# Hybrid decoder step on one core: the cache attention's value products moved into the next prompt block

## The chip, the core and the metric

The kernel runs on one core of one Trainium2 chip. TensorE (PE) multiplies matrices, VectorE (DVE), ScalarE (ACT) and GpSimd (POOL) do the element work, SyncE (SP), ACT and POOL issue transfers. The metric is the time of one execution in device microseconds (us); lower is better.

## The reference

One step of a two-layer decoder for a prompt of 1024 tokens and eight sample requests of one token each. Layer 0 is an mLSTM, layer 1 is multi-head latent attention over 8 heads, each followed by a dense feed-forward network. The change touches layer 1 alone, and there two things: the attention of the prompt over itself, and the attention of each sample over its cache of 8192 rows, which lie in pages at random places:

```python
def one_seq(args):
    ql, qr, cn, krn, pages = args
    c_all = jnp.concatenate([cache_latent[layer_idx, pages].reshape(past, KV_LORA), cn], axis=0)
    kr_all = jnp.concatenate([cache_k_rope[layer_idx, pages].reshape(past, QK_ROPE), krn], axis=0)
    s = jnp.einsum('qhc,kc->hqk', ql, c_all) + jnp.einsum('qhr,kr->hqk', qr, kr_all)
    s = jnp.where(mask, s.astype(jnp.float32) * MLA_SCALE, -jnp.inf)
    p = jax.nn.softmax(s, axis=-1)
    return jnp.einsum('hqk,kc->qhc', p.astype(c_all.dtype), c_all)
```

The cached latent rows (256 wide) serve as keys and, after the softmax, as values.

## The kernel before

**Prompt attention.** `attention` walks over 8 heads and, in each, over 4 blocks of 256 queries: 32 blocks, called slots (`slot = h * 4 + i`). `prompt(h, G, ...)` traces one block: the score matmuls (L1693 to L1700, into PSUM tiles `sc`), the softmax on DVE and ACT (L1701 to L1718), the transposes of the probabilities (L1731), their split into two float32r halves (`wh`, `wl`, L117, L118, and L128 to L130 where POOL helps) and the products with the values (L1751). Between blocks stand pieces of `head_ops(h + 1)`, which makes the next head's keys `kt` (matmuls of 512 columns, L134 to L136) and, for every second head, the values `vt` of two heads. Its weights come by SP into `swh` and `swl`, which have one buffer each: the load for the keys of an odd head can start when the last product with the value weights before it is done. The keys of the next head are made behind the first block of the current head.

**Cache attention.** `sample_units(b, first)` is a generator: each of the 8 samples is done in two units, 16 in all (numbered 0 to 15 below), and each unit in two halves (`u`), one half per slot, with no half in slots 0, 30 and 31 and two in 3, 11 and 27. A half gathers 2048 cache rows: POOL issues two indirect transfers of 1 MB into `nat` (L1840) and two small ones into `nrp` (L1841). DVE transposes them in 32 x 32 squares (L1848, five instructions of 1024 elements a partition), and PE multiplies them by the queries (L1855) into the left half of a PSUM tile `ss`. After the second half comes the unit's softmax on DVE and ACT (L1860 to L1871), 16 small copies that spread the probabilities over `pz` (L1876, half on DVE, half on ACT), and the value products (L1880, 32 matmuls, each of them two passes in the trace) into the right half of `ss`; DVE adds them to `acc` (L1881). After the second unit of a sample follows the merge: a chain of four small PE steps (L1887, L1892, L1897, L1904) with DVE and ACT steps in between.

**What sets the order.** A scheduler lays the traced instructions out, engine by engine, by its own model of when each is ready; each engine then works through its list in order and waits where an operand is late. Two handles steer it here. `high_priority(offset=SOON)` raises instructions, so that they are taken as soon as the model has them ready (the cache's scores and values). `issue_after(ins)` puts what a block traces behind `ins` on the same engine, with no wait for its end.

**Buffers that tie the units together.** `nat` has four buffers, so the gathers of unit n+2 wait for the value products of unit n. `ss` has two buffers. `pz`, `sS` and `acc` have one.

Of the kernel before, what the change touches and what calls it, by code (L numbers as in the profile page):

```python
# [12 lines left out]
AF = mybir.ActivationFunctionType  # L13
ALU = mybir.AluOpType
# [4 lines left out]
P = 128  # L19
# [72 lines left out]
class Kern:  # L92
# [15 lines left out]
    def t(self, pool, shape, tag, dt=F32, bufs=None):  # L108
        self.n += 1
        return pool.tile(shape, dt, tag=tag, name=f"{tag}{self.n}", **({"bufs": bufs} if bufs else {}))  # L110
# [1483 lines left out]
    def attention(self, ckh, ckl, kk, kl, cqp, cq):  # L1594
# [16 lines left out]
        ahead = {}  # L1611

# [10 lines left out]
        def head_ops(h):  # L1623
# [8 lines left out]
            yield r  # L1632
            for c in range(2):
                cs = slice(c * cw, (c + 1) * cw)
                ps = ps1()
                for j in range(2):
                    self.mm3(ps, wh[:, j], wl[:, j], ckh[:, j, cs], ckl[:, j, cs], j == 0, j == 1)
                split(kt[:, 0, cs], kt[:, 1, cs], ps, [P, cw])
# [29 lines left out]
        def prompt(h, G, kt, vt):  # L1668
# [10 lines left out]
            for i in (2 * G, 2 * G + 1):  # L1679
# [8 lines left out]
                for c in range(nb):  # L1688
# [10 lines left out]
                    if last:  # L1699
                        mm(o[:, w - P:], mk[:, 0], mk[:, 1], start=False, stop=True)  # L1700
# [17 lines left out]
                pn.append(px)  # L1718
            for j0 in range(0, nk, 4):
# [52 lines left out]
        for h in range(8):  # L1772
# [11 lines left out]
            for i, G in enumerate(range(4) if h % 2 == 0 or h == 7 else range(3, -1, -1)):  # L1784
# [8 lines left out]
                if slot == 30:  # L1793
                    next(units, None)
                    pr.release()
                    self.pc.release()
                    out = self.mla_out()
                    next(out)
# [15 lines left out]
    def sample_units(self, b, first):  # L1814
# [6 lines left out]
        psb = lambda: self.mmt("ss")  # L1821
# [7 lines left out]
        ss = psb()  # L1829
# [47 lines left out]
        with self.tc.high_priority(offset=SOON):  # L1877
            for i in range(8):
                for j in range(4):
                    nc.tensor.matmul(psV[32 * j:32 * j + 32], pz[:, j, i], keys[i // 4][:, j * 4 + i % 4], start=i == 0, stop=i == 7)  # L1880
        V.scalar_tensor_tensor(self.acc, self.acc, al, psV, op0=ALU.mult, op1=ALU.add)  # L1881
        if not first:

            ps = psb()
            m = t([P, 1], "m", 1)
            V.tensor_scalar(m, nb, -1.0, None, op0=ALU.mult)
            nc.tensor.transpose(ps[0:1, 0:P], m, self.ident)  # L1887
            mn = t([1, 8], "mn", 1)
            V.reduce_max(mn, ps[0:1, 0:P].rearrange("o (x h) -> o h x", h=8), axis=AX.X)
            mc = t([P, 256], "sS", 1)[0:1, :P].rearrange("o (x h) -> o x h", h=8)  # L1890
            V.tensor_copy(mc, mn.unsqueeze(1).to_broadcast([1, 16, 8]))
            nc.tensor.matmul(ps[:, P:P + 1], mc.rearrange("o x h -> o (x h)"), self.ones[0:1, 0:1], start=True, stop=True)  # L1892
            fac = t([P, 1], "fac", 2)
            V.tensor_tensor(fac, m, ps[:, P:P + 1], op=ALU.subtract)
            nc.scalar.activation(fac, fac, AF.Exp)
            V.tensor_scalar(self.lrow, self.lrow, fac, None, op0=ALU.mult)
            nc.tensor.matmul(ps[:, 256:257], self.ct[:, C_SL:C_SL + P], self.lrow, start=True, stop=True)  # L1897
            rl = t([P, 1], "rl", 2)
            V.reciprocal(rl, ps[:, 256:257])
            w = t([P, 8], "w0", 2)  # L1900
            V.tensor_scalar(w, self.ct[:, C_SL:C_SL + 8], rl, fac, op0=ALU.mult, op1=ALU.mult)
            ps = psb()
            for f in range(2):
                nc.tensor.matmul(ps[:, f * 8:f * 8 + 8], self.acc[:, f * P:(f + 1) * P], w, start=True, stop=True)  # L1904
            V.tensor_copy(self.olat[:, :, :, b], ps[:, 0:16].rearrange("p (f h) -> p f h", f=2))
# [164 lines left out]
```

## Time and profile before

| | |
|---|---|
| three timed runs | 2610.46, 2617.35, 2619.27 us (median 2617.35) |
| the profiled execution | 2606.56 us, span of its instructions 2604.6 us |
| PE busy | 2496.4 us, 96% of the span |
| DVE, ACT, POOL busy | 1858.4, 1327.5, 573.7 us |
| HBM traffic | 146 GB/s over the span |

The profiled execution is 0.4% under the median of the timed runs, so numbers of its trace are set against its own time. The stage that the change touches is the attention of layer 1, from about 1331 to 1810 us of the span. In rows of groups and of the timeline, "out<-in" names tiles, the number in brackets or behind the second bar is the time for which the engine sat idle just before, with what ended it.

### The profile page before, as it was taken

What the parts mean: (1) busy time and instruction counts of PE and PEld (TensorE: products, weight loads), DVE (VectorE), ACT (ScalarE), POOL (GpSimd) and SP (SyncE); (2) the same over time, 40 slices, a digit from 0 to 9 for tenths busy, and PEclk for the clock granted to TensorE, in tenths of its full rate; (3) what the DMA queues carried; (4) which work ended last, traced back from release to release, by engine and by line L of the source; (5) the groups of instructions that cost most, each with busy time, mean ns of one, the idle gap of its engine ahead of it and who ended that gap; (6) DMA issues with size and microseconds to landing.
All of it is one profiled execution on the core that took longest, in us unless ns stands there. A gap on an engine that the chain in (4) does not pass through costs nothing. (4 is left out here: it accounts for less than half of the span.)

```text
span 2604.6 us, 54290 instructions
## 1 busy us (share of the span) xinstructions
PE 2496.4 (96%) x21151; PEld 2361.3 (91%) x21151; DVE 1858.4 (71%) x4491; ACT 1327.5 (51%) x3281; POOL 573.7 (22%) x588
## 2 busy tenths in 40 slices
PE   8998988999999999999988888998999999999998
PEld 8998987999999999999977676777899999999998
DVE  4345669898777777666658776777498877777765
ACT  4122334456655656554445454656356656556543
POOL 1000102301111111112435445451211111111102
PEclk9999999999999999999999999999999999999999
DMA  6133555526666665555568667674635666665663
GB/s 195 41 64 82 150 140 126 162 74 135 119 129 124 129 129 115 113 154 165 177 230 290 219 222 249 223 254 127 206 106 111 119 129 129 129 128 115 121 139 112
DMA packets 343127, 382.87 MB, mean 147 GB/s; under 512 B 23465, under 2 KB 275502, under 8 KB 334550
## 3 DMA queue, kind: packets, MB, share of 16 engines
q0 software_dynamic: 58688, 180.35, 29.7%
q1 hardware_dynamic: 258982, 182.30, 23.5%
q10 hardware_dynamic: 25200, 16.75, 2.6%
q8 instruction: 166, 2.72, 0.4%
q14 instruction: 91, 0.75, 0.1%
HBM read 253.63 MB, written 125.70 MB: 146 GB/s over the span
## 5 line engine op out<-in xcount | busy, mean ns | idle before, releaser
L1187 POOL DMA_DIRECT2D x_d<-wl x72 | 86.8, 1205 | 996.1 <-DVE wl L1186 359.7
L117 ACT ACTIVATE wh<-wr 128x512 fp32r<-128x512 f32 (+2 forms) x167 | 133.3, 800 | 192.9 <-PE mm L135 111.4
L1848 DVE STREAM_TRANSPOSE tt<-nat 128x1024 f32<-128x1024 f32 x128 | 153.6, 1222 | 23.4 <-DMA nat<-in_cache_latent_dram,idx 13.8
L118 DVE TENSOR_TENSOR wl<-wr,wh 128x1024 fp32r<-128x1024 f32 (+2 forms) x80 | 92.9, 1162 | 37.3 <-ACT wh L117 36.3
L134 PE MATMUL mm<-zh,wh 128*128 128x344 f32 x320 | 104.2, 326 | 6.0 <-DVE ot L467 6.0
L117 ACT ACTIVATE b<-u 128x256 fp32r<-128x256 f32 (+1 forms) x252 | 98.5, 415 | 20.5 <-PE ss L136 6.3
L118 DVE TENSOR_TENSOR b<-u,b 128x256 fp32r<-128x256 f32 (+1 forms) x252 | 103.5, 424 | 6.8 <-ACT b L117 5.4
L1187 POOL DMA_DIRECT2D x_d<-st x72 | 104.4, 1450 | 4.8 <-DVE dC L118 3.8
L135 PE MATMUL mm<-zl,wh 128*128 128x344 f32 x320 | 103.8, 324 | 0.0
L136 PE MATMUL mm<-zh,wl 128*128 128x344 f32 x320 | 103.7, 324 | 0.0
L118 DVE TENSOR_TENSOR wh<-S,wh 128x512 fp32r<-128x512 f32 x108 | 74.6, 691 | 34.6 <-ACT wh L117 34.3
L1855 PE MATMUL ss<-tt,qbd 128*32 128x128 f32 x2560 | 86.6, 276 | 4.2 <-DVE tt L1848 2.3
L117 ACT ACTIVATE wh<-S 128x512 fp32r<-128x512 f32 x108 | 67.9, 629 | 44.4 <-PE sc L136 32.1
L1855 PEld LDWEIGHTS ss<-tt,qbd 128*32 128x32 f32 x2560 | 69.7, 110 | 16.8 <-DVE tt L1848 10.8
L1751 PE MATMUL mm<-wh,vt 128*128 128x256 f32 (+1 forms) x320 | 76.5, 301 | 7.5 <-ACT wh L117 5.5
L134 PE MATMUL sc<-zh,wh 128*128 128x344 f32 x256 | 82.6, 323 | 0.9 <-ACT wh L117 0.8
L136 PE MATMUL sc<-zh,wl 128*128 128x344 f32 x256 | 82.0, 320 | 0.7 <-DVE wl L118 0.7
L135 PE MATMUL sc<-zl,wh 128*128 128x344 f32 x256 | 81.9, 320 | 0.0
L1880 PE MATMUL ss<-nat,pz 128*32 128x256 f32 x1024 | 67.3, 393 | 12.3 <-ACT pz L1876 11.7
L1710 ACT ACTIVATE wr<-sc,mx,rqt 128x512 f32<-128x512 f32 (+2 forms) x96 | 64.3, 674 | 20.4 <-DVE mx L1705 10.0
L1840 POOL DMA_INDIRECT nat<-in_cache_latent_dram,idx x64 | 60.6, 947 | 62.6 <-PE ss L1880 49.0
L1751 PEld LDWEIGHTS mm<-wh,vt 128*128 128x128 f32 x320 | 56.6, 199 | 19.4 <-ACT wh L117 9.9
(1078 smaller groups left out, 10650.7 us busy)
## 6 DMA issues: line engine op xcount, KB each, us to landing
wr<-in_ffn_w_gate_up_dram SPq DMA_DIRECT2D x96, 512.0 KB
x_d<-st POOLq DMA_DIRECT2D x72, 520.0 KB, 8.0
x_d<-wl POOLq DMA_DIRECT2D x72, 512.0 KB, 6.0
dr<-in_ffn_w_down_dram SPq DMA_DIRECT2D x72, 256.0 KB
wr<-in_mlstm_w_in_dram SPq DMA_DIRECT2D x24, 512.0 KB
wr<-in_mlstm_w_out_dram SPq DMA_DIRECT2D x16, 512.0 KB
q<-qn_d SPq DMA_DIRECT2D x28, 256.0 KB
wr<-in_mla_w_o_dram SPq DMA_DIRECT2D x14, 512.0 KB
```

The lines of the kernel that those rows point to most:

```text
L117: ins = nc.scalar.activation(hi, src, AF.Copy)
L118: self.low = e.tensor_tensor(lo, src, hi.bitcast(F32), op=ALU.subtract)
L134: mm(ps, wh, xh, start=start, stop=False, **kw)
L135: mm(ps, wh, xl, start=False, stop=False, **kw)
L136: self.last = mm(ps, wl, xh, start=False, stop=stop, **kw)
L1187: nc.gpsimd.dma_start(self.x_d[:, 2 * dp:2 * dp + 2, 512 * i:512 * i + 2 * PW[i]], st[i], accum_op=ALU.add)
L1710: nc.scalar.activation(px[:, ks], o, AF.Exp, bias=mx[:, 0:1], scale=f, accum_out=sm[:, c:c + 1])
L1751: nc.tensor.matmul(o, x, y, start=i == 0, stop=i == len(ops) - 1)
L1840: nc.gpsimd.indirect_dma_start(out=nat[:, s].rearrange("p s c -> p (s c)"), out_offset=None, in_=lat, in_offset=ix)
L1848: V.transpose(out=tt, in_=src.rearrange("p s (c i) -> p c s i", i=32))
L1855: nc.tensor.matmul(psS[32 * j:32 * j + 32, u * P:u * P + P], self.qbd[:, b, cb], tt[:, c, 4 * j:4 * j + 4].rearrange("p s k -> p (s k)"), ...
L1880: nc.tensor.matmul(psV[32 * j:32 * j + 32], pz[:, j, i], keys[i // 4][:, j * 4 + i % 4], start=i == 0, stop=i == 7)
```

## The change

1. The value products and all that follows them in a unit (`acc`, the merge) become a function `values`, kept in `self.due`. It is called when the next prompt block has traced its scores and its softmax, just ahead of its transposes; if no block comes in between (the slots with two halves, slot 30), it is called at the start of the next half. 
2. The value matmuls stay raised and are also queued behind `self.qk`, the last score matmul of the newest block.
3. The merge no longer takes two PSUM tiles of its own; it uses parts of the unit's `ss`.
4. The keys of odd heads are made behind the second block of the head before, not behind the first (`if h % 2: yield`), and the key matmuls of all heads but the first are queued behind `self.qk`.

No matmul, copy or transfer is added or left out.

```diff
         late = []
         ahead = {}
+        self.due = None
...
             yield r
+            if h % 2:
+                yield
             for c in range(2):
                 cs = slice(c * cw, (c + 1) * cw)
                 ps = ps1()
                 for j in range(2):
-                    self.mm3(ps, wh[:, j], wl[:, j], ckh[:, j, cs], ckl[:, j, cs], j == 0, j == 1)
+                    with self.tc.issue_after(self.qk) if h else nullcontext():
+                        self.mm3(ps, wh[:, j], wl[:, j], ckh[:, j, cs], ckl[:, j, cs], j == 0, j == 1)
...
                     if last:
-                        mm(o[:, w - P:], mk[:, 0], mk[:, 1], start=False, stop=True)
+                        self.qk = mm(o[:, w - P:], mk[:, 0], mk[:, 1], start=False, stop=True).ins
...
                 pn.append(px)
+            if self.due:
+                self.due()
             for j0 in range(0, nk, 4):
...
                 if slot == 30:
                     next(units, None)
+                    if self.due:
+                        self.due()
                     pr.release()
...
-        psb = lambda: self.mmt("ss")
+        if self.due:
+            self.due()
         if first:
...
-        ss = psb()
+        ss = self.mmt("ss")
...
-        with self.tc.high_priority(offset=SOON):
-            for i in range(8):
-                for j in range(4):
-                    nc.tensor.matmul(psV[32 * j:32 * j + 32], pz[:, j, i], keys[i // 4][:, j * 4 + i % 4], start=i == 0, stop=i == 7)
-        V.scalar_tensor_tensor(self.acc, self.acc, al, psV, op0=ALU.mult, op1=ALU.add)
-        if not first:
-
-            ps = psb()
...
+        acc, lrow = self.acc, self.lrow
+
+        def values():
+            self.due = None
+            with self.tc.high_priority(offset=SOON), self.tc.issue_after(self.qk):
+                for i in range(8):
+                    for j in range(4):
+                        nc.tensor.matmul(psV[32 * j:32 * j + 32], pz[:, j, i], keys[i // 4][:, j * 4 + i % 4], start=i == 0, stop=i == 7)
+            V.scalar_tensor_tensor(acc, acc, al, psV, op0=ALU.mult, op1=ALU.add)
+            if not first:
...
+        self.due = values
         yield
```

The order that the scheduler makes of it shows at three places. In the rows, `ss` with a number is one unit's PSUM tile, `sc` the scores of a prompt block, `mm` a PSUM tile of transposes, products or keys. The new lines are 4 to 13 higher: L1697 to L1704 are scores, L1737 transposes, L1757 products of a prompt block, L1864 the cache's scores, L1893 its values.

PE at the value products of unit 4 (`ss_17795` before, `ss_17769` after). Before, they stand in the middle of the scores of unit 5 and of a prompt block's transposes and products:

```order
L1731 MATMUL mm_17900<-ct_66,wr_17870 128x128
L1731 MATMUL mm_17900<-ct_66,wr_17885 128x128 x2
L1698 MATMUL sc_18050<-kl_14540,qrr_17853 128x512
L1855 MATMUL ss_18148<-tt_18337,qbd_16086 32x128 x8
L1855 MATMUL ss_18148<-tt_18333,qbd_16086 32x128 x8
L1855 MATMUL ss_18148<-tt_18335,qbd_16086 32x128 x5
L1880 MATMUL ss_17795<-nat_17796,pz_15354 32x256 x16
L1880 MATMUL ss_17795<-nat_17924,pz_15354 32x256 x16
L1855 MATMUL ss_18148<-tt_18335,qbd_16086 32x128 x3
```

After, on the same engine, they follow the last score of a block (`sc_18044`) and precede its transposes:

```order
L1700 MATMUL sc_18037<-kk_14539,qrr_17827 128x512
L1702 MATMUL sc_18037<-kl_14540,qrr_17827 128x512
L1697 MATMUL sc_18044<-kt_16819,q_17826 128x256
L1698 MATMUL sc_18044<-kt_16819,q_17826 128x256
L1699 MATMUL sc_18044<-kt_16819,q_17826 128x256
L1700 MATMUL sc_18044<-kk_14539,qrr_17827 128x256
L1702 MATMUL sc_18044<-kl_14540,qrr_17827 128x256
L1704 MATMUL sc_18044<-mk_15350 128x128
L1893 MATMUL ss_17769<-nat_17770,pz_15354 32x256 x16
L1893 MATMUL ss_17769<-nat_17920,pz_15354 32x256 x16
L1737 MATMUL mm_18094<-ct_66,wr_18029 128x128
```

What moved: the values went behind more of the queue, from the middle of one group of small work to the gap between a block's scores and its transposes.

PE at the first scores of unit 8 (`ss_19289` before, `ss_19281` after), whose gathers wait for the values of unit 6. Before, they come behind the last step of the merge of unit 7 (L1897, L1904):

```order
L1897 MATMUL ss_19187<-lrow_18469,ct_66 128x1
L1694 MATMUL sc_19393<-kt_18532,q_19209 128x256
L1695 MATMUL sc_19393<-kt_18532,q_19209 128x256
L1696 MATMUL sc_19393<-kk_14539,qrr_19210 128x256
L1698 MATMUL sc_19393<-kl_14540,qrr_19210 128x256
L1700 MATMUL sc_19393<-mk_15350 128x128
L1751 MATMUL mm_19036<-wh_19017,vt_17399 128x128
L1904 MATMUL ss_19205<-w_19203,acc_18466 128x8
L1855 MATMUL ss_19289<-tt_19300,qbd_16086 32x128 x8
L1855 MATMUL ss_19289<-tt_19296,qbd_16086 32x128 x8
```

After, they come two dozen matmuls of a prompt block and the second-half scores of unit 7 behind the values of unit 6, inside the products of that block (`mm_18621`):

```order
L1704 MATMUL sc_18983<-mk_15350 128x128
L1697 MATMUL sc_18998<-kt_17653,q_18759 128x512
L1698 MATMUL sc_18998<-kt_17653,q_18759 128x512
L1757 MATMUL mm_18621<-wh_18602,vt_17631 128x128
L1699 MATMUL sc_18998<-kt_17653,q_18759 128x512
L1864 MATMUL ss_19281<-tt_19292,qbd_16086 32x128 x8
L1864 MATMUL ss_19281<-tt_19288,qbd_16086 32x128 x8
L1864 MATMUL ss_19281<-tt_19290,qbd_16086 32x128 x8
L1757 MATMUL mm_18621<-wl_18603,vt_17631 128x128
```

What moved: the first scores of a unit stand earlier, and nearer to the values of the unit two before it.

PE at the keys of head 5 (`mm_19426` before, `mm_19607` after). Before, they stand in the products of the first block of head 4, which use `vt_18905`:

```order
L1751 MATMUL mm_19416<-wl_19407,vt_18905 128x128
L1751 MATMUL mm_19416<-wh_19406,vt_18905 128x128
L1751 MATMUL mm_19416<-wl_19407,vt_18905 128x256
L1751 MATMUL mm_19416<-wh_19406,vt_18905 128x256
L134 MATMUL mm_19426<-ckh_14547,swh_19364 128x512
L135 MATMUL mm_19426<-ckl_14548,swh_19364 128x512
```

After, they stand behind the products of the second block (`mm_19591`):

```order
L1757 MATMUL mm_19591<-wh_19572,vt_18899 128x256
L1757 MATMUL mm_19591<-wh_19572,vt_19046 128x256
L1757 MATMUL mm_19591<-wl_19573,vt_19046 128x256
L1757 MATMUL mm_19591<-wh_19572,vt_19046 128x256
L134 MATMUL mm_19607<-ckh_14547,swh_19356 128x512
L135 MATMUL mm_19607<-ckl_14548,swh_19356 128x512
```

What moved: one block of a prompt lies between the last product with `vt` weights and the keys.

More of the change, by code (lines that the diff above doesn't have):

```diff
@@ L1876, in sample_units @@
                 e(pz[32 * kb:32 * kb + 32, j, :, 8 * kb:8 * kb + 8], pT[32 * j:32 * j + 32, kb])
-        with self.tc.high_priority(offset=SOON):
-            for i in range(8):
-                for j in range(4):
-                    nc.tensor.matmul(psV[32 * j:32 * j + 32], pz[:, j, i], keys[i // 4][:, j * 4 + i % 4], start=i == 0, stop=i == 7)
-        V.scalar_tensor_tensor(self.acc, self.acc, al, psV, op0=ALU.mult, op1=ALU.add)
-        if not first:
-            ps = psb()
[L1885 to L1905, printed above, removed]
@@ new lines, in sample_units @@
+        acc, lrow = self.acc, self.lrow
[7 more added lines that the diff above has]
+            if not first:
+                m = t([P, 1], "m", 1)
+                V.tensor_scalar(m, nb, -1.0, None, op0=ALU.mult)
+                nc.tensor.transpose(ss[0:1, 0:P], m, self.ident)
+                mn = t([1, 8], "mn", 1)
+                V.reduce_max(mn, ss[0:1, 0:P].rearrange("o (x h) -> o h x", h=8), axis=AX.X)
+                mc = t([P, 256], "sS", 1)[0:1, :P].rearrange("o (x h) -> o x h", h=8)
+                V.tensor_copy(mc, mn.unsqueeze(1).to_broadcast([1, 16, 8]))
+                nc.tensor.matmul(ss[:, P:P + 1], mc.rearrange("o x h -> o (x h)"), self.ones[0:1, 0:1], start=True, stop=True)
+                fac = t([P, 1], "fac", 2)
+                V.tensor_tensor(fac, m, ss[:, P:P + 1], op=ALU.subtract)
+                nc.scalar.activation(fac, fac, AF.Exp)
+                V.tensor_scalar(lrow, lrow, fac, None, op0=ALU.mult)
+                nc.tensor.matmul(ss[:, 256:257], self.ct[:, C_SL:C_SL + P], lrow, start=True, stop=True)
+                rl = t([P, 1], "rl", 2)
+                V.reciprocal(rl, ss[:, 256:257])
+                w = t([P, 8], "w0", 2)
+                V.tensor_scalar(w, self.ct[:, C_SL:C_SL + 8], rl, fac, op0=ALU.mult, op1=ALU.mult)
+                for f in range(2):
+                    nc.tensor.matmul(ss[:, 384 + f * 8:392 + f * 8], acc[:, f * P:(f + 1) * P], w, start=True, stop=True)
+                V.tensor_copy(self.olat[:, :, :, b], ss[:, 384:400].rearrange("p (f h) -> p f h", f=2))
```

## The prediction

> **What bounds the kernel now.** The page first, then the stage that the change touches, as one window (its ends and length, the busy time of PE, its weight loads, DVE, ACT and POOL, the granted clock, the DMA share and GB/s).
>
> ```profile
> span 2604.6 us, 54290 instructions
> ...
> PE 2496.4 (96%) x21151; PEld 2361.3 (91%) x21151; DVE 1858.4 (71%) x4491; ACT 1327.5 (51%) x3281; POOL 573.7 (22%) x588
> ```
> ```profile
> 1331.00:1810.00 479.00, 421.23 (x5230) 334.50 (x5228) 346.29 (x774) 265.43 (x700) 221.00 (x219) 0.96 0.66 229
> ```
>
> TensorE bounds the program. In the stage it is busy for 421.2 of 479.0 us, so it idles 57.8 us there, and its granted clock averages 0.96. The change adds and removes no work, so it can only move these idle times and the clock. What PE waits for, by groups of its instructions in the stage (idle before them behind the second bar), and four rows of who waited for whom (us, times, longest):
>
> ```profile
> L1855 PE MATMUL ss<-tt,qbd 128*32 128x128 f32 x2560 | 86.6, 276 | 4.2 <-DVE tt L1848 2.3 <-DVE sm L1713 0.5
> ...
> L1880 PE MATMUL ss<-nat,pz 128*32 128x256 f32 x1024 | 67.3, 393 | 12.3 <-ACT pz L1876 11.7 <-issue 0.4
> ...
> L1731 PE MATMUL mm<-ct,wr 128*128 128x128 f32 x273 | 49.2, 289 | 12.1 <-ACT spl L129 5.0 <-ACT wr L1715 4.0 <-ACT ot L1754 2.3
> ...
> L134 PE MATMUL mm<-ckh,swh 128*128 128x512 f32 x28 | 12.5, 447 | 5.6 <-DMA swh<-uw_d 4.6 <-ACT ot L1754 1.0
> ...
> L1904 PE MATMUL ss<-w,acc 128*128 128x8 f32 x32 | 5.2, 240 | 1.4 <-DVE w L1901 1.4
> ...
> L1892 PE MATMUL ss<-ones,sS 1*128 1x1 f32 x16 | 3.0, 256 | 1.0 <-DVE sS L1891 0.9
> ```
> ```profile
> POOL nat L1840 <- PE ss L1880: 49.0, 12, 6.5
> ...
> DVE tt L1848 <- DMA nat<-in_cache_latent_dram,idx: 13.8, 5, 4.1
> ...
> PE ss L1904 <- DVE w L1901: 1.4, 2, 0.7
> ...
> PE ss L1892 <- DVE sS L1891: 0.9, 1, 0.9
> ```
>
> The values (L1880) wait 11.7 us for `pz`, the keys 4.6 us for their weights. The first two rows of the waits show the return path: POOL's gathers wait for the values, DVE's transposes for the gathers. PE itself hardly waits for transposes (2.3 us).
>
> **Values later: the gain.** How much PE work covers a unit's softmax, I count in the two orders (instructions between its last score and its first value product) and price at the spacing of starts in a stretch at full clock; small matmuls by busy time over count, 86.6/2560 and 67.3/1024 us a pass.
>
> ```profile
> 1649.97 0.87 PE L1731 MATMUL mm<-ct,wr 128*128 128x128 f32 x6
> 1650.60 0.48 PE L1693 MATMUL sc<-kt,q 128*128 128x512 f32 x1
> 1650.92 0.40 PE L1694 MATMUL sc<-kt,q 128*128 128x512 f32 x1
> 1651.15 0.40 PE L1695 MATMUL sc<-kt,q 128*128 128x512 f32 x1
> ...
> 1658.49 0.28 PE L1751 MATMUL mm<-wl,vt 128*128 128x256 f32 x1
> 1658.61 0.40 PE L1751 MATMUL mm<-wh,vt 128*128 128x256 f32 x2
> ```
>
> That is 0.11 us a transpose, 0.23 for 512 columns, 0.12 for 256. Units 2 to 14 have 2.6 to 14.6 us of cover before and 9.5 to 28.2 after; I cost their waits at nothing then. Units 0, 1 and 15 gain none: 5.1 becomes 4.6, 4.6 becomes 4.5, 5.6 becomes 3.3.
>
> ```profile
> 1388.06 3.70 PE L1880 MATMUL ss<-nat,pz 128*32 128x256 f32 x62 [1.54 <-ACT pz L1876]
> ```
> ```profile
> 1494.73 5.36 PE L1880 MATMUL ss<-nat,pz 128*32 128x256 f32 x64 [3.78 <-ACT pz L1876]
> ```
> ```profile
> 1789.03 0.63 PE L1880 MATMUL ss<-nat,pz 128*32 128x256 f32 x4 [0.91 <-ACT pz L1876]
> ```
>
> Unit 0 keeps 1.5 + 0.5, unit 15 keeps 0.9 + 2.3, unit 1 gets 0.1: 5.3 us together. So 11.7 - 5.3 = **6.4 us saved**; at best 11.7, at worst nothing, if DVE and ACT are later with `pz` by as much.
>
> **Keys one block later: the gain.** The longest wait is that of head 5's keys:
>
> ```profile
> 1616.16 0.77 PE L134 MATMUL mm<-ckh,swh 128*128 128x512 f32 x1 [3.83 <-DMA swh<-uw_d]
> ```
>
> Their load starts when the last `vt` product ends and needs about that long. A whole block now lies between (two dozen matmuls or more, over 4 us), so **4.6 us** go. The splits of odd keys on POOL move with them and are needed two blocks later only. SP's loads keep their place, so no `q` load is queued behind a longer wait.
>
> **The clock.** The two longest waits, 3.78 and 3.83 us, are followed by slow stretches (granted clock third from the end of a row):
>
> ```profile
> 1616.10:1620.00 3.90, 3.84 (x9) 3.10 (x10) 0.00 (x0) 0.91 (x2) 0.00 (x0) 0.50 0.63 246
> ...
> 1494.70:1500.10 5.40, 5.37 (x74) 4.55 (x78) 3.79 (x5) 0.24 (x1) 1.15 (x2) 0.70 0.01 3
> ```
>
> 0.50 x 3.9 + 0.30 x 5.4 = **3.6 us** go with them. After the 1.54 us wait the 62 passes took 3.70 us, the usual 0.06 each, so short waits cost nothing more. I charge 1.8 us for each new wait of 3.8 us or longer. (The Trainium skill, "TensorE: Matmul & The Clock Gate", Part 1, puts the limit at an idle window of about 3.4 us, after which the clock is halved; that speaks against the change, since it would make some of the new waits below dearer. No wait here lies between 1.54 and 3.78 next to a measured clock to say where the limit is; by the page's figure the forecast is unchanged, since its only long wait is over both.)
>
> **Gathers later: the cost.** POOL issues the gathers of unit n+2 when the values of unit n have read the first `nat`, and the first scores of n+2 need both transfers and three transposes. Two such cases, each engine's timeline:
>
> ```profile
> 1498.65 0.96 POOL L1840 DMA_INDIRECT nat<-in_cache_latent_dram,idx  x1 [6.33 <-PE ss L1880]
> 1499.91 0.94 POOL L1840 DMA_INDIRECT nat<-in_cache_latent_dram,idx  x1 [0.30 <-issue]
> ```
> ```profile
> 1507.93 1.25 DVE L1848 STREAM_TRANSPOSE tt<-nat 128x1024 f32<-128x1024 f32 x1 [2.30 <-DMA nat<-in_cache_latent_dram,idx]
> ...
> 1509.19 1.24 DVE L1848 STREAM_TRANSPOSE tt<-nat 128x1024 f32<-128x1024 f32 x1
> ```
> ```profile
> 1555.94 0.48 DVE L1881 SCALAR_TENSOR_TENSOR acc<-acc,al,ss 128x256 f32<-128x256 f32 x1 [0.41 <-PE ss L1880]
> ...
> 1564.60 3.50 DVE L1848 STREAM_TRANSPOSE tt<-nat 128x1024 f32<-128x1024 f32 x3 [1.74 <-DMA nat<-in_cache_latent_dram,idx]
> ```
> ```profile
> DMA to landing us min/median/max: 5.6/7.4/9.9
> ```
>
> From the values' end (1494.73 + 5.36 = 1500.09) to the first transpose 7.8 us; in the second case (1555.9 to 1564.6) 8.7. With the middle, 8.3, two transposes of 1.24 and 0.4 for a small operation between, PE can start the scores **11.2 us** after the values' end. The work in between, by the orders, for n = 0 to 13: before 17.9, 15.0, 19.8, 16.7, 18.8, 23.3, 22.2, 23.2, 23.4, 15.7, 24.7, 15.5, 22.5, 17.1 us; after 11.5, 12.1, 8.4, 12.8, 10.8, 14.0, 5.9, 8.2, 9.6, 10.9, 8.2, 8.2, 9.6, 10.6. So the slack that hides the gathers today is gone. Real time runs longer than this count:
>
> ```profile
> L1855 PE MATMUL ss<-tt,qbd x2560: 270/273/423, 1367.0 to 1779.7; 128*32 128x128 f32 x197
> ```
> ```profile
> L1880 PE MATMUL ss<-nat,pz x1024: 376/379/636, 1388.1 to 1793.7; 128*32 128x256 f32 x171
> ```
>
> From 1367.0 to 1793.7 are 427 us, against 334 by the count: a factor 1.28, of which I keep 1.2, since some waits go. Times 1.2, only n = 2, 6, 7, 10 and 11 fall short of 11.2, by 1.1, 4.1, 1.4, 1.4 and 1.4: **9.4 us of new waits**, and **1.8** for the long one. With the factor 1 it is 21.6; with all transfers at the fastest landing 1.3. DVE stands in the same wait, and a block's reductions and splits behind it, but PE has stopped at the scores by then, so I count it once.
>
> **Merges.** In units 9, 13 and 15 two of the four joints now have only some six transposes or four scores of cover (0.6 to 1.1 us). The waits seen at such joints are 1.4 in two and 0.9 in one, 0.8 each: six of them, less the 2.4 seen today, **+2.4 us**; between -2.4 and +5. POOL's clearing of `acc` waits for the merge as before. The two PSUM tiles fewer cost nothing: the first scores of n+2 now wait only for unit n's own tile, whose merge is over by then.
>
> **Sum**: -6.4 - 4.6 - 3.6 + 9.4 + 1.8 + 2.4 = -1.0 us against the profiled 2606.6. The median of the runs is 10.8 above that; on its scale 2616.4, in round terms **2616 us**.
>
> **Rivals.** *Gathers in time (faster).* If both transfers land like the fastest (5.6 us after issue), the need is 1.25 + 5.6 - 1.4 + 2.9 = 8.4 us after the values' end, and only n = 6 waits, 1.3. Then -14.6 + 1.3 + 2.4 = -10.9, and if the values also fill three of the 4.0 us for which transposes wait for the softmax (L1731, `wr`), -14: **2603 us**. For it: fewer transfers may share the time; against it: the median landing. (By the Trainium skill, "DMA: Bandwidth & Descriptors", Anatomy of one DMA, a transfer takes 2.0 us plus bytes/436e3; for 1 MB I estimate 4.4 us, which leads to this rival. The trace's shortest is 5.6, so it does not bear the page out.)
>
> *Scores in front of late gathers (slower).* If some DVE work lies between landing and third transpose, 1.6 us more, the need is 12.8: waits of 2.7, 5.7, 3.0, 1.3, 3.0, 3.0, 1.3 and 0.1, 20.1 in all, and -14.6 + 20.1 + 1.8 + 2.4 = +9.7: 2627 us. With 13.7 (landing near the worst) 28.5 us, four of them long: +23.5, 2641 us. It decides from a need of about 12.5 on. For it: the long row of 13.8 us on DVE, and that five gaps have shrunk to 5.9 to 8.4.
>
> *No effect where it is meant.* After 1494.73 shows that DVE and ACT can take long to fill `pz` whatever stands on PE; if the values wait as today, -8.2 + 13.6 = +5.4, 2623 us, within the measurement.
>
> **Chances.** About 0.3% (7.9 us) is what a measurement of this kernel can tell from no change. Forecast and third rival 0.37 (own range 2609 to 2625), gathers in time 0.33, late gathers 0.30. From these: faster 0.33, same 0.37, slower 0.30. The range reaches from 2600, below the second case's 2603, to 2640, near the end of the third's.
>
> **What would show it.** Right: values waiting for `pz` only in units 0, 1 and 15; no wait of L134 for `swh`; new waits of the scores for DVE's transposes, longest at unit 8 (4 us), and DVE waiting longer for `nat`. Wrong: scores without waits (the first rival), or a wait at most units and the clock at a half behind several (the second). The prediction fails in another way if waits of the prompt's own products, which I left as they are, shift by more than the terms above.

## The result, and the profile after

Nine runs of each kernel: before 2613.69 us in the median (2609.62 to 2619.67), after **2600.93 us** (2597.15 to 2605.0), ratio 0.9948 with a 95% interval of 0.9935 to 0.996. The change gains 0.5%, 12.8 us between the medians. The forecast was 2616; the time lies inside the range, near its faster end and near the first rival's 2603. The profiled execution of after took 2597.15 us, that of before 2606.6: 9.4 us between these two. In some of the later comparisons both kernels take longer (the kernel before 2635 to 2640 us instead of 2612), so ratios are compared there.

The page of after:

```profile
span 2595.3 us, 54269 instructions
...
PE 2492.7 (96%) x21151; PEld 2360.5 (91%) x21151; DVE 1859.5 (72%) x4491; ACT 1328.1 (51%) x3281; POOL 573.6 (22%) x588
```

A window with fixed ends holds different work in the two kernels, so the stage is now cut by its work: from the first prompt score of the stage to the end of its last prompt product. Its length, and the busy time of each engine in it, before:

```profile
1331.21:1827.30 496.09, 437.91 (x5318) 348.91 (x5317) 358.25 (x803) 276.44 (x729) 224.28 (x223) 0.96 0.65 225
```

and after:

```profile
1329.65:1815.11 485.46, 433.53 (x5324) 347.44 (x5323) 361.60 (x803) 277.02 (x729) 225.01 (x223) 0.95 0.67 230
```

The stage is 10.6 us shorter. TensorE idles 51.9 us in it (485.46 - 433.53) instead of 58.2, and is busy 4.4 us less with the same products. The stage begins 1.6 us earlier, and 2.9 us are lost behind it (780.2 instead of 777.3 us from its end to the span's end; a wait of 3.1 us of the output's first product for `wh` is new there).

The groups of TensorE in the stage after, idle time behind the second bar:

```profile
L1864 PE MATMUL ss<-tt,qbd 128*32 128x128 f32 x2560 | 88.1, 280 | 10.9 <-DVE tt L1857 8.9 <-DVE sm L1717 0.9 <-DVE olat L1915 0.2
L1893 PE MATMUL ss<-nat,pz 128*32 128x256 f32 x1024 | 63.4, 392 | 4.4 <-ACT pz L1885 4.4
...
L1737 PE MATMUL mm<-ct,wr 128*128 128x128 f32 x288 | 51.5, 292 | 5.4 <-ACT spl L129 2.9 <-ACT wr L1719 2.2
...
L134 PE MATMUL mm<-ckh,swh 128*128 128x512 f32 x28 | 11.3, 403 | 4.7 <-ACT ot L1760 4.7
...
L1914 PE MATMUL ss<-w,acc 128*128 128x8 f32 x32 | 5.1, 268 | 1.8 <-DVE w L1912 1.8
```

Against the rows of before: the values wait 4.4 us instead of 12.3, the prompt's transposes 5.4 instead of 12.1. The unit's scores wait 10.9 instead of 4.2. The keys' wait for their weights is gone, but they wait 4.7 instead of 1.0 us for ScalarE's copy `ot`, which holds their PSUM tile. The waits of all engines in the same stage (us, times, longest):

```profile
DVE tt L1857 <- DMA nat<-in_cache_latent_dram,idx: 24.3, 10, 6.6
...
POOL nat L1849 <- PE ss L1893: 13.5, 6, 6.4
...
PE sc L1697 <- ACT wr L1714: 6.6, 4, 5.5
...
PE ss L1903 <- DVE sS L1902: 5.4, 4, 3.0
```

VectorE waits 24.3 us for the gathers (13.8 before), and the merges' second joint (L1903) 5.4 us (0.9 before). One wait is gone that the prediction did not cost. In the same view of before it reads:

```profile
PE sc L1696 <- DMA qrr<-qr_d: 3.4, 4, 2.4
```

With 1.3 us for `q` beside it, loads of the blocks' queries cost 4.8 us before and nothing after.

The return path is best seen at unit 12, on GpSimd, VectorE and TensorE in turn:

```profile
1664.14 0.95 POOL L1849 DMA_INDIRECT nat<-in_cache_latent_dram,idx  x1 [1.14 <-PE ss L1893]
```
```profile
1665.69 0.47 DVE L1894 SCALAR_TENSOR_TENSOR acc<-acc,al,ss 128x256 f32<-128x256 f32 x1
...
1674.39 2.37 DVE L1857 STREAM_TRANSPOSE tt<-nat 128x1024 f32<-128x1024 f32 x2 [6.59 <-DMA nat<-in_cache_latent_dram,idx]
```
```profile
1676.81 2.42 PE L1864 MATMUL ss<-tt,qbd 128*32 128x128 f32 x48 [2.41 <-DVE tt L1857]
```

Unit 10's values have ended when VectorE adds them to `acc` at 1665.69. The third transpose ends at 1676.76, and the scores start 11.1 us behind the values, close to the predicted need of 11.2.

Unit 12 is the only unit whose first scores wait in this way. Its 2.4 us are a small part of the 8.9 us for which the scores wait for transposes: 2.6 us stand at unit 0, ahead of which there are no values, and most of the rest in second halves of units, 1.8 us in unit 3 and 1.3 in unit 7:

```profile
1443.69 1.08 PE L1864 MATMUL ss<-tt,qbd 128*32 128x128 f32 x32 [1.84 <-DVE tt L1857]
```

VectorE waits for no transfer ahead of these two; it is at work on other steps and other transposes.

### The profile page after: what moved, and what is told of

It reads as the page before. It is cut to its first block, busy times and chain, and to the rows that moved or that the text cites. A ratio compares the mean times of both kernels' runs of the same rounds, so it can differ in the third digit from the quotient of the medians.

```text
span 2595.3 us, 54269 instructions
## 1 busy us (share of the span) xinstructions
PE 2492.7 (96%) x21151; PEld 2360.5 (91%) x21151; DVE 1859.5 (72%) x4491; ACT 1328.1 (51%) x3281; POOL 573.6 (22%) x588
## 4 chain that ended last, share of the span: by engine, by line
PE 69%; DVE 9%; DMA 6%; issue 2%; ACT 2%; POOL 2%; SPq 0%; ACTq 0%; POOLq 0%; DVEq 0%
PE sc L134 13%; PE sc L136 13%; PE sc L135 13%; PE mm L134 5%; PE mm L136 5%; PE mm L135 5%; DMA nat<-in_cache_latent_dram,idx 2%; PE ss L134 2%; PE ss L135 2%; PE ss L136 2%; DVE tt L1857 2%; PE ss L1864 2%; PE ss L1893 1%; DVE wl L118 1%; PE mm L1757 1%
## 5 line engine op out<-in xcount | busy, mean ns | idle before, releaser
L1857 DVE STREAM_TRANSPOSE tt<-nat 128x1024 f32<-128x1024 f32 x128 | 155.4, 1228 | 28.9 <-DMA nat<-in_cache_latent_dram,idx 24.3
L1864 PE MATMUL ss<-tt,qbd 128*32 128x128 f32 x2560 | 88.1, 280 | 10.9 <-DVE tt L1857 8.9
L1864 PEld LDWEIGHTS ss<-tt,qbd 128*32 128x32 f32 x2560 | 70.5, 112 | 26.4 <-DVE tt L1857 18.5
L1757 PE MATMUL mm<-wh,vt 128*128 128x256 f32 (+1 forms) x320 | 74.7, 297 | 8.4 <-ACT wh L117 7.1
L1850 POOL DMA_INDIRECT nrp<-in_cache_k_rope_dram,idx x64 | 61.4, 959 | 57.9 <-DVE tt L1857 24.5
L877 POOL TENSOR_TENSOR ss<-ss,sq 128x512 f32<-128x512 f32 (+2 forms) x36 | 50.7, 1407 | 106.0 <-ACT sq L876 106.0
L1757 PEld LDWEIGHTS mm<-wh,vt 128*128 128x128 f32 x320 | 56.0, 198 | 18.1 <-ACT wh L117 11.2
```

The lines of the kernel that those rows point to most:

```text
L877: (V if d == KT - 1 else nc.gpsimd).tensor_tensor(SS[:, cs], SS[:, cs], sq, op=ALU.add)
L1757: nc.tensor.matmul(o, x, y, start=i == 0, stop=i == len(ops) - 1)
L1850: nc.gpsimd.indirect_dma_start(out=nrp[:, s].rearrange("p s c -> p (s c)"), out_offset=None, in_=rop, in_offset=ix)
L1857: V.transpose(out=tt, in_=src.rearrange("p s (c i) -> p c s i", i=32))
L1864: nc.tensor.matmul(psS[32 * j:32 * j + 32, u * P:u * P + P], self.qbd[:, b, cb], tt[:, c, 4 * j:4 * j + 4].rearrange("p s k -> p (s k)"), ...
```

## The experiments

The kernel before took 2635 us beside e1 to e4, 2612.5 beside e5 to e8, 2636 beside e9 to e11 and 2640 beside e12. Ratios from the 2612 us comparisons (the first result too) are set against each other, and so are those from the others. How far ratios of different comparisons can be trusted shows in the changed kernel itself: 0.9948 in the first result and 0.9927 in e5, both of the first kind. Differences of 0.2% between comparisons are thus not read.

**The two halves, the tile and the queue.** e1 leaves the keys as before and moves the values alone:

```diff
-            if h % 2:
-                yield
...
-                    with self.tc.issue_after(self.qk) if h else nullcontext():
-                        self.mm3(ps, wh[:, j], wl[:, j], ...)
+                    self.mm3(ps, wh[:, j], wl[:, j], ...)
```

> The change without its part on the keys (odd heads' keys stay behind the first block, no key matmul is queued behind the scores). Theory 'cover' (the gain is the values' wait for pz and the transposes' wait for the softmax, both covered by the values' new place): ratio 0.995 to 0.997 to the kernel before, values waiting for pz 4 to 5 us, transposes waiting 5 to 7 us as in the changed kernel; the wait of 4.6 us for the key weights comes back. Theory 'keys' (the odd keys' load is the gain): ratio 0.999 to 1.001. Theory 'free tile' (the merge no longer takes PSUM tiles, so scores start earlier): the same as the first here, told apart by the next runs.

Measured: 2611.57 us, ratio 0.9907 (0.9885 to 0.993). The values alone carry the gain, and more of it than any of the theories said. The waits are not those of the first theory: the values wait 0.9 us for `pz`, the prompt's transposes 10.3 in all, against 12.1 in the profile of before. The keys' wait for `swh` did not come back either: it went with the values' order.

e2 is the kernel before with both edits of the keys and nothing else.

> The kernel before with the odd heads' keys one block later and key matmuls queued behind the scores, nothing else. Theory 'cover': the 4.6 us wait for the key weights goes, but about 2 to 5 us of it come back as a wait for the PSUM tile that the copy of a block's result frees, as in the changed kernel: ratio 0.998 to 1.000. Theory 'keys': ratio 0.995 to 0.997.

Measured: 2643.26 us, ratio 1.0021 (1.0005 to 1.0038). The keys' move alone gains nothing and may cost 0.2%; blocks wait for their query loads instead of for keys. The longest group of its waits in the stage:

```profile
PE sc L1696 <- DMA q<-qn_d: 13.4, 5, 7.6
```

e3 is the kernel before with the merge in the unit's own tile `ss`:

```diff
-            ps = psb()
             m = t([P, 1], "m", 1)
...
-            nc.tensor.transpose(ps[0:1, 0:P], m, self.ident)
+            nc.tensor.transpose(ss[0:1, 0:P], m, self.ident)
```

> The kernel before with the merge done in the unit's own PSUM tile, nothing else: values stay where they are traced, covers of the values 2.7 to 18.9 us (mean 9.8 against 7.4 before, 15.6 after), first scores of a unit 8.9 to 28.4 us of work behind the values two units before (mean 14.6 against 19.7 and 10.1). Theory 'free tile': ratio 0.995 to 0.997. Theory 'cover': the values' wait falls by less than half, ratio 0.998 to 1.000.

Measured: 2665.21 us, ratio 1.0114 (1.0094 to 1.0134), slower than either theory said. The tile alone is no free edit: with it the order of the instructions changes. In e3 the unit's scores wait 11.0 us for transposes and the blocks' scores 12.1 for ScalarE:

```profile
PE sc L1693 <- ACT wr L1710: 12.1, 9, 5.8
...
PE ss L1855 <- DVE tt L1848: 11.0, 12, 3.7
```

e4 is the changed kernel without the queue behind the block's last score:

```diff
-            with self.tc.high_priority(offset=SOON), self.tc.issue_after(self.qk):
+            with self.tc.high_priority(offset=SOON):
```

> The changed kernel without queueing the values behind the block's last score: they are still traced inside the next block and raised, so the scheduler takes them when its model has pz ready. Cover by the order 3.9 to 24.9 us, mean 9.5. Theory 'cover': part of the wait for pz returns (7 to 10 us in all against 4.4), ratio 0.996 to 0.999 to the kernel before. Theory 'free tile' or 'keys': as the changed kernel, 0.994 to 0.996.

Measured: 2649.85 us, ratio 1.005 (1.0032 to 1.0069), slower than either theory said. One line decides the sign: without it 1.005, with it 0.9907 in the same comparison (e1, where the keys stay) and 0.989 in another (e12). The values wait again in many units, and the blocks for their queries:

```profile
PE sc L1697 <- DMA q<-qn_d: 7.6, 2, 6.6
PE ss L1893 <- ACT pz L1885: 4.9, 8, 1.7
```

**Control, and the keys again.** e5 is the changed kernel itself.

> The changed kernel as it is, beside the next three on the same chip. Both theories: the ratio 0.995 of the first comparison, within 0.0025, so that the half without the keys' move (0.991 on another chip) can be set against it.

Measured: 2597.2 us, ratio 0.9927 (0.991 to 0.9943). Its waits in the stage repeat those of the first profile in kind, with sizes off by up to 3 us:

```profile
PE ss L1864 <- DVE tt L1857: 6.9, 6, 3.0
...
PE ss L1903 <- DVE sS L1902: 5.6, 4, 3.3
PE mm L134 <- ACT ot L1760: 4.8, 2, 2.5
...
PE ss L1893 <- ACT pz L1885: 2.0, 3, 0.9
```

e6 is the kernel of e1 in the same comparison.

> The move of the values alone, with the odd heads' keys where they were. Theory 1 (the keys' move pays as the two traces say: 4.6 us of load waits against 2.3 more of waits for ScalarE): 2.3 us, 0.1%, above the changed kernel, ratio 0.996. Theory 2 (the keys' move costs, since it puts the odd keys' products behind a block's last score and their tile behind ScalarE's copies): 0.3 to 0.4% below the changed kernel, ratio 0.991, as on the other chip.

Measured: 2598.02 us, ratio 0.9943 (0.9927 to 0.9959), 0.8 us above e5 with overlapping intervals. The second theory (the keys' move costs 0.3 to 0.4%) falls; the first is not excluded, and a gain of 2 us is not shown. The move exchanges one wait for another: without it a query load is waited for, 3.6 us; with it the odd keys wait for `ot`, 4.8 us (e5) instead of 1.1.

```profile
PE sc L1697 <- DMA qrr<-qr_d: 3.6, 2, 3.3
PE ss L1890 <- ACT pz L1882: 2.9, 1, 2.9
...
PE mm L134 <- ACT ot L1757: 1.1, 1, 1.1
```

**Are the new waits time on the path?** e7 raises every step of the merges:

```diff
             if not first:
-                m = t([P, 1], "m", 1)
-                ...
+                with self.tc.high_priority(offset=SOON):
+                    m = t([P, 1], "m", 1)
+                    ...
```

> The changed kernel with all steps of the merges (VectorE, ScalarE and TensorE) raised like the values. Theory 1 (the merges' waits, 8.5 us after against 2.6 before, are time on the path, since VectorE does a block's work ahead of them): most of the 5.9 us come back, waits of the merges under 3 us, ratio 0.993. Theory 2 (TensorE stands at these joints while the gathers are under way, so the scores after them wait longer instead): no change, 0.995, with waits of the scores up by as much as the merges' go down.

Measured: 2603.03 us, ratio 0.9959 (0.9944 to 0.9975), 5.8 us above e5. The second theory has the mechanism, but the kernel got slower where it said no change: the merges' waits fall from 6.8 to 2.5 us, and those of the scores rise from 8.7 to 22.9. (The profiled execution is the slowest of its seven, 2614.45 us.)

```profile
L1864 PE MATMUL ss<-tt,qbd 128*32 128x128 f32 x2560 | 88.6, 280 | 22.9 <-DVE tt L1857 21.7 <-DVE sm L1717 0.4
...
L1904 PE MATMUL ss<-ones,sS 1*128 1x1 f32 x16 | 3.0, 256 | 0.6 <-DVE sS L1903 0.4
```

e8 puts one more instruction on GpSimd ahead of each unit's gathers:

```diff
+            if u == 0:
+                nc.gpsimd.memset(nat[:, 0:8], 0.0)
```

> The changed kernel with one more instruction on GpSimd per unit: half of the first nat tile is cleared ahead of its gather (about 1.8 us by the 2.24 us that clearing 128x2560 takes). Theory 1 (the return path from a unit's values over the gathers and transposes to the scores of two units later is on the path in about nine units, where the scores started 0 to 1.3 us after their third transpose): 12.7 us more, ratio 1.000, waits of the scores for transposes at 15 us or more. Theory 2 (the path has slack; the waits of the scores seen after are those of a few late blocks): within 3 us of the changed kernel, 0.995 to 0.996.

Measured: 2601.92 us, ratio 0.9949 (0.9933 to 0.9966), 4.7 us above e5. The delay is 1.81 us per unit, and the scores' waits rise by 16 us, from 8.7 to 25.0, more than the 12.7 of the first theory:

```profile
L1846 POOL MEMSET nat<- 128x2048 f32 x16 | 29.0, 1810 | 17.4 <-PE ss L1895 17.3
```
```profile
PE ss L1866 <- DVE tt L1859: 21.2, 23, 4.5
```
```profile
1333.45:1822.40 488.95, 430.79 (x5324) 341.28 (x5323) 366.01 (x803) 276.91 (x729) 253.23 (x239) 0.95 0.67 228
```

In this run the first scores start 0.1 us or less behind their third transpose in 13 of the 14 units that have values ahead of them. So the path has hardly any slack left, as the prediction held, but the time is nearer to the second theory: a microsecond of wait there cost about 0.3 us (4.7 / 16.3; by the scatter of five runs of each kernel, 0.1 to 0.6). The extra instruction also delays GpSimd's splits, but products wait for those no longer than in e5 (0.4 against 0.5 us). The row of the stage says where the rest is: it is 2.8 us longer than in e5 (486.16), with 10.1 us more idle time (58.2 against 48.1) and 7.3 us less busy time for the same products. Other waits shrink (those of the prompt's products 13.3 to 9.5, of the keys 4.8 to 2.8), and the clock is at a half for 13 windows of 3.41 us instead of 18 (8.5 us less lost).

**Other ways to place the same work.** e9 gives each merge two PSUM tiles of its own again:

```diff
+                ps = self.mmt("ss")
                 m = t([P, 1], "m", 1)
...
-                nc.tensor.transpose(ss[0:1, 0:P], m, self.ident)
+                nc.tensor.transpose(ps[0:1, 0:P], m, self.ident)
```

> The changed kernel with each merge back in two PSUM tiles of its own (the ring of two that the units use). Theory 1 (the tiles only save PSUM turns, as the prediction had it: they cost nothing): within 0.15% of the changed kernel, 0.9927 on the same scale. Theory 2 (a merge in the next unit's slot takes the ring's next tiles, so the scores of two units later wait for the merge's end; in the order of instructions the values' cover falls from 15.6 to 7.6 us in the mean and the scores come 20 instead of 10 us after the values): the waits for pz come back (5 to 9 us), those of the scores vanish, ratio 0.996 to 1.002.

Measured: 2619.57 us, ratio 0.9942 (0.9925 to 0.996). The changed kernel in a like comparison is e12 with 0.9891, but in a comparison of its own and on another chip: the own tile is worth 0.5% by these ratios, 0.3% by the times, and the two stages differ by 1.1 us only (504.4 and 503.3). That it gains something here is likely and not shown; that it does not cost the 1.1% that it cost alone (e3) is. The waits for `pz` are 3.7 us against 1.6 in e12, those for transposes 5.2 against 7.7; the direction is that of the second theory, the sizes are smaller than it said.

```profile
PE ss L1864 <- DVE tt L1857: 5.2, 10, 2.2
PE ss L1893 <- ACT pz L1885: 3.7, 7, 0.9
```

e10 does not raise the scores of a unit's first half:

```diff
-                with self.tc.high_priority(offset=SOON):
+                with self.tc.high_priority(offset=SOON) if u else nullcontext():
```

> The changed kernel with the scores of a unit's first half not raised: the order then puts 16 us of other work instead of 10 between the values of a unit and the scores of two units later, and 7.6 instead of 15.6 between a unit's last score and its values. Theory 1 (both paths weigh the same): waits of the scores fall by 7 to 9 us, those for pz rise by 5 to 8, ratio within 0.15% of the changed kernel's 0.9927. Theory 2 (the return path over the gathers is the dearer one): ratio 0.990 or less. Theory 3 (the gain was cover for the softmax): 0.996 or more.

Measured: 2628.08 us, ratio 0.9966 (0.9953 to 0.9979), 8.5 us above e9 in the same comparison and 0.75% above e12. The time is the third theory's, the waits are not: the scores hardly wait for transposes (3.4 us), but the values wait for `pz` only 0.6 us longer than in e12 (2.2 against 1.6), so it is not their cover that is missed. The stage's idle time (53.6 us) is even below e12's (57.4), but its busy time is 15 us longer (460.9 against 445.9). The unit's scores take 110.8 instead of 98.2 us of it, and run in 106 separate pieces instead of 82. In e12 the start behind the last score of a piece mostly comes 0.20 us after it, that behind a group of four inside a piece 0.09 us; at 0.11 us for each piece more, I estimate that the pieces make 2.6 of the 12.6 us. What makes up the rest is left open.

```profile
PE ss L1864 <- DVE tt L1857: 3.4, 7, 1.8
```

e11 lets the unit's scores start with the rope part, whose gather does not wait for the values:

```diff
-                    for cp, tt in parts[-1:] + parts[:-1]:
+                    for cp, tt in parts:
...
-                                   start=cb == 2, stop=cb == 5)
+                                   start=cb == 8, stop=cb == 7)
```

> The changed kernel with the scores' column parts in the order of their transposes (rope part first) instead of the last one first, so that TensorE has the rope part, whose gather is not held up by the values, before the first nat transpose. Theory 1 (the scores' waits for the late gathers are on the path): the rope part's 16 matmuls and one nat part's run inside the wait and the need falls by one transpose, waits of the scores 3 to 6 us less, ratio 0.990 to 0.992. Theory 2 (raised as they are, the rope parts come straight behind the values and TensorE then stands in the middle of the scores instead of ahead of them): no change, 0.993, or more idle time than before, 0.995.

Measured: 2618.22 us, ratio 0.9932 (0.9914 to 0.995), 0.4% above e12 by the ratio and 0.2% by the time. The order is as the second theory said: the rope part comes straight behind the values and TensorE stands in the middle of the scores, 16 times instead of 10. But these waits are not where the time goes: all idle time of the stage is 48.6 us, below e12's 57.4, and the busy time is 12 us longer (457.9 against 445.9). As in e10 it is the scores that take longer, 111.1 us against 98.2, in 131 pieces.

```profile
PE ss L1864 <- DVE tt L1857: 12.8, 16, 1.5
```

**The changed kernel beside a slower "before".**

> The changed kernel once more, since the kernel before took 2612 us in one of the three comparisons and 2635 and 2636 in the two others, and the half without the keys' move gave 0.9943 in the first kind and 0.9907 in the other. Theory 1 (the ratio belongs to the kernel): 0.993 to 0.995 whatever the time of before. Theory 2 (where the kernel before takes 2635 us, TensorE's extra stalls of about 1 us between small products make the change worth more): 0.990 to 0.992 there, and then the orders with other tiles (0.9942), with scores not raised (0.9966) and with the rope part first (0.9932) all lose to it; beside a kernel before of 2612 us this run tells nothing new.

Measured: 2612.75 us beside 2640.29, ratio 0.9891 (0.9874 to 0.9907). It is the second theory's case: beside a kernel before of 2640 us the change is worth 1.1%, not 0.5 to 0.7%, and e9, e10 and e11 lose to it, while the values alone (e1, 0.9907) can't be told from it. The profile shows what is different there: TensorE stalls at the scores without a wait for any engine or transfer that the trace knows, and the scores are busy for 98.2 us instead of 88.1 (first profile) and 91.1 (e5).

```profile
PE ss L1864 <- issue: 9.7, 21, 1.0
...
PE ss L1864 <- DVE tt L1857: 7.7, 10, 2.8
```
```profile
1617.15 0.38 PE L1864 MATMUL ss<-tt,qbd 128*32 128x128 f32 x2 [1.01 <-issue]
```

In the first profile of after and in those of e5 to e8 the scores have no such row. The profiles of e1 to e4 and of e9 to e12 all have them (6.5 to 15.1 us at the scores). What causes the stalls is not shown; e5 to e8 and e9 to e11 ran on a chip of the same number, so the chip alone does not decide. Why the change is worth more there can't be read, since no profile of the kernel before was taken in such a comparison.

## Why the prediction was right or wrong

The terms against the idle times of two profiles of the changed kernel (the first, and e5's), all in the stage cut by its work:

| term | predicted, us | first profile | e5 |
|---|---|---|---|
| values for `pz` (12.3 in all) | -6.4 | -7.9 | -10.3 |
| keys (all their products 7.0) | -4.6 | -2.3 | -2.2 |
| half-speed windows, lost time (22.2) | -3.6 + 1.8 | +3.4 | +8.5 |
| scores behind late gathers (all waits of the scores 4.1) | +9.4 | +6.8 | +4.6 |
| merges (2.6) | +2.4 | +5.9 | +4.2 |
| prompt's transposes (12.1) | not costed | -6.7 | -6.1 |
| blocks' scores (9.2; query loads 4.8 of it) | not costed | -2.6 | -2.8 |
| prompt's products (10.8) | not costed | +0.6 | +2.5 |
| all idle time (58.2) | | -6.3 | -10.1 |

The clock's row lies mostly in the busy time, not in the idle rows. Stage, start and rest together make -9.4 us in the profiled pair; the sum said -1.0. The last 3.4 us of the 12.8 are scale: the nine runs put the median of before 7.1 us above its profiled execution, not 10.8, and that of after 3.8 above its own.

- **Values later**: right in kind, a little too small. The place behind the block's last score decides: e4 loses 1.4% against e1 in the same comparison. But the values' own wait is the smaller part of that. Of the 36.9 us by which the stage of e4 is longer than that of e1 (538.1 against 501.2), 7.7 are idle time ahead of the values, 11.3 idle time ahead of the blocks' scores, and 20.9 are busy time, with 27 windows at half speed instead of 15; the other idle times are 2.9 less in sum. Of the units named, 0 and 1 wait as said (3.0 and 0.4 us), 15 does not, 14 does (0.9):

```profile
1385.26 1.76 PE L1893 MATMUL ss<-nat,pz 128*32 128x256 f32 x12 [3.04 <-ACT pz L1885]
```

- **Keys later**: the wait for `swh` went as said, but the step "4.6 us go" forgot who else the moved products meet. Their PSUM tile is held by ScalarE's copy of the block before:

```profile
1616.33 0.50 PE L134 MATMUL mm<-ckh,swh 128*128 128x512 f32 x1 [2.18 <-ACT ot L1760]
```

 Alone the move gains nothing (e2), and beside the values' move no gain is shown (e6). The sentence that no query load is queued behind a longer wait is not borne out by e2, where the blocks wait 13.4 us for `q`; how much of that is older than the edit can't be told there.
- **Gathers later**: the mechanism was right and the charge was not. The need of 11.2 us is met to 0.1 us at unit 12, and e8 shows that the path has no slack in most units. Of the five units said to wait (4, 8, 9, 12, 13) only 12 does, by 2.4 us (3.0 in e5), where 9.4 were charged; the other 4.4 of the +6.8 us in the table stand at other places (unit 0 and second halves). Unit 8 was to wait longest, 4.1 us; its first scores do not wait at all, since TensorE had already lost time between the values and them:

```profile
1545.00:1556.90 11.90, 8.33 (x112) 6.11 (x110) 8.36 (x18) 6.91 (x20) 7.03 (x7) 0.89 0.83 288
```

 3.6 of these 11.9 us are six waits for VectorE and ScalarE, and the clock is below full. So the step that failed is the factor of 1.2 by which I stretched the counted work; between the values and the scores of units 6 to 15, 137 us passed where 96.0 were counted, a factor of 1.43 (1.40 without unit 12's own wait, 2.0 for unit 8). It was taken low "since some waits go", but waits came as well. The need was not the same everywhere either: in units 9, 11 and 13 the third transpose ended 13.2, 14.3 and 13.6 us behind the values, past even the second rival's 12.8, and TensorE still came to the scores 0.1 to 0.2 us after it. The error of the factor hid the error of the need.
- **Merges**: +2.4 was within its bounds (-2.4 to +5) only by e5; the first profile has +5.9. e7 speaks for it that this hardly matters: with the merges' waits nearly gone TensorE waits longer at the scores.
- **The clock**: the step "short waits cost nothing more" failed. Waits of 2.4 and 3.0 us are each followed by a window at half speed (last section). The charge belonged to more waits than the one of 3.8 us: before already had 13 such windows in the stage, 22.2 us, and the working looked at two places. The trace of before does have a wait between 1.54 and 3.78 us beside a measured clock: the blocks' scores wait 2.36 us for a query load, and the clock behind that wait stays full (third from the end of the row):

```profile
1363.20:1367.00 3.80, 2.40 (x11) 1.82 (x11) 3.51 (x4) 0.00 (x0) 1.26 (x2) 1.00 1.01 393
```

- **What was left as it was** failed most: transposes and query loads gave 11.5 us that no term held, of which 3.3 went again into the blocks' scores waiting for ScalarE. The prediction had named this as another way in which it would fail. For the loads the cause is shown in part: e4, with the values no longer behind the block's last score, waits 8.7 us for queries, where the first profile of after, e5 and e12 show no such wait; e6 shows that the keys' move has a part in it (3.6 us come back without it). For the transposes it is only argued: values that stand between a block's scores and its transposes cover the block's softmax too, for which the first rival had 3 us. But the transposes of e4 wait 3.4 us, less than those of e12 (7.7), and with the values moved alone they wait 10.3 in e1 and 6.6 in e6, so what made them quicker between the first pair of profiles stays open.

The likeliest case was thus not the one that came, and the first rival's time (2603) came by another way than the gathers being in time. That the time lies inside the range owes much to luck: gains and costs that were missed cancelled in part.

## What to carry to other kernels

When a deferred piece of TensorE work is placed between another block's scores and its transposes, queue it behind the last score, since raising it alone turned a gain into a loss here, and count the block's loads among what it covers. A wait that a trace shows is not a price: 16 us more of waits at one line cost 4.7 us, and taking 4 us of waits away from another cost 5.8. Where a return path closes a loop (values, gathers, transposes, scores), its length is what to predict, and the elapsed time between its ends, not the work counted between them, is what to compare it with.

## What the runs showed of the hardware

The granted clock changes on a fixed grid of 3.41 us, and one window at half speed takes away 1.7 us of full-speed time. How much of the window before TensorE stood idle tells more than how long a single wait was. Windows of after on that grid (the length, PE's busy time and count, and the granted clock third from the end):

```profile
1472.40:1475.80 3.40, 0.52 (x3) 0.51 (x4) 2.50 (x7) 0.67 (x3) 2.78 (x3) 1.00 1.02 374
1475.90:1479.30 3.40, 3.40 (x16) 3.24 (x15) 3.40 (x10) 1.22 (x5) 0.00 (x0) 0.50 0.98 387
...
1673.90:1677.30 3.40, 0.99 (x21) 0.57 (x23) 2.91 (x4) 0.67 (x2) 3.32 (x3) 0.99 1.03 387
1677.30:1680.70 3.40, 3.40 (x48) 3.02 (x36) 2.52 (x5) 1.02 (x4) 0.00 (x0) 0.51 0.89 353
1680.70:1684.10 3.40, 3.38 (x51) 2.91 (x51) 3.40 (x8) 2.37 (x6) 0.97 (x1) 1.00 0.07 20
```

A wait of 2.97 us (a merge at 1475.28) and the 2.41 us of unit 12 each fill most of a window, and the next window runs at a half. Over the 14 profiles of this case, without the first 15 us of the program, a window that follows one at full speed ran at a half in all 84 cases in which TensorE had been idle for 60% or more of the one before, in 97 of 233 with 35 to 60%, and in 44 of 9963 with less. So a wait of 2.4 us can cost nothing (before, at 1363) or 1.7 us (after, unit 12), by how it and its neighbours fall on the grid; this may be part of why profiles of one kernel differ by some microseconds.

Idle time does not explain all of it. In 36 of those 44 cases TensorE had been busy for over 95% of the window before, most of them at about the same four places of the program. One is at the start of the stage, here in after:

```profile
1332.50:1335.90 3.40, 3.40 (x30) 3.04 (x30) 0.61 (x3) 1.27 (x5) 0.99 (x2) 1.00 0.55 196
1335.90:1339.30 3.40, 3.40 (x26) 2.43 (x25) 1.19 (x6) 1.52 (x4) 2.80 (x4) 0.50 0.65 234
```

What halves the clock there is not shown. (The Trainium skill, "TensorE: Matmul & The Clock Gate", Part 1, gives a free-running window of 3413 ns, which these rows bear out. The same page of the Trainium skill advises, in its section "Why this matters for your kernels", to leave no idle gaps of over about 3 us; that is too mild for this kernel, where 2.4 us were enough, and so is the limit of 3.4 us that the prediction took from Part 1.)

The orders without queued values also spend more of the stage at half speed: 26 or 27 windows in e2, e3 and e4 against 14 to 17 in e1 and e9 to e12, beside kernels before of like time. At 1.7 us a window that is 15 to 22 us; their stages are 21 to 49 us longer (535.6 to 549.8 us against 501.2 to 514.5).
